# ScalarE in place of VectorE for modulated values and V's weight splits in the first projection

## The chip, the cores and the metric

The kernel runs on one core of one Trainium2 chip. The metric is the device time of one execution in microseconds (us); for a kernel, the median of its runs. The engines are named as in the profile: PE is TensorE (matmuls; PEld are its weight loads), DVE is VectorE, ACT is ScalarE, POOL is GpSimd, and SP issues the DMA transfers.

## The reference

One layer of an encoder, batch 1, 1024 tokens, model width 1024, all in float32. What matters for this change is the beginning:

```python
mod = jnp.dot(jax.nn.silu(c), w_ada[l]) + b_ada[l]
sh_a, sc_a, g_a, sh_m, sc_m, g_m = jnp.split(mod, N_MOD, axis=-1)
h = modulate(rmsnorm(x, g_attn_norm[l]), sh_a, sc_a)
proj = jnp.dot(h, w_in[l])
q_lat, kv_lat, k_rope, ca_qkv = jnp.split(proj, split_pts, axis=-1)
...
x = x + g_a[:, None, :] * mixed
...
x = x + g_m[:, None, :] * jnp.dot(jax.nn.silu(gate) * val, w_down[l])
```

`modulate(h, shift, scale)` is `h * (1 + scale) + shift`. The columns of `w_in` feed two kinds of attention (latent attention, "MLA", and chunked attention over a key band), whose outputs go through one output projection; a gated MLP with a causal convolution follows.

## The kernel before

**Splits.** A float32 product is made on PE as three products of parts. Each operand is split into a rounded part ("hi", type fp32r) and the remainder ("lo", the value minus hi). `gemm3` then issues hi x hi (L154), hi x lo (L155) and lo x hi (L156) into the same PSUM tile. `hi_of(eng, o, i)` makes a rounded part: on ACT as a copy (L77), on POOL, or on DVE as a cast (L81). `lo_of` makes the remainder as a subtraction (L84).

**The opening stage.** The 1024 model dimensions are eight blocks of 128, d = 0 to 7; the 1024 tokens are two halves of 512, h = 0 and 1. The modulation (shift and scale) is not there at the start: its weights `w_ada_a` come in four pairs of blocks, each as four tiles `adaw` of 512 KB (five buffers), and `ada_pair` adds them up on DVE, weighted by silu(c), in eight steps per pair (L271, then L273 seven times) into `adacc`. For each block d, PE sums `adacc` over the partitions with matmuls of one column into `p_ada` (L288), and DVE makes the two columns of `modT` from it (L291 to L293). Two blocks share one pair: blocks 2 and 3 need the second pair, 4 and 5 the third, 6 and 7 the fourth.

For each block and each half, `mod_transpose` has PE transpose four tiles of the normalized x into one PSUM tile `ht_ps` (L228; one buffer for each half, named T and pv). ACT makes the rounded modulated part into `hT[:, 0]` (L231). The full-precision modulated value `hv` is made from the same PSUM tile by the engine that the argument `veng` names: ACT (L234) or DVE (L236). The remainder `hT[:, 1]` is their difference (L237), on DVE or POOL by the argument `leng`. Before the change, half 0 has `hv` on ACT and the remainder on POOL; half 1 has both on DVE. The PSUM buffer of a half is free for the next block when both readings of it are done.

Then PE adds this block's part of the first Q/K projection for all eight token tiles: 24 matmuls with 128x256 outputs into `qk0` (two PSUM tiles, one for each half). When all eight blocks are done, ACT copies `qk0` (L344) and squares it (L346), DVE sums the squares (L349), POOL makes the inverse roots, and DVE multiplies.

**V's weights.** `wv0_load` loads the eight raw chunks of V's weights (`wvr`, 128x256 each) on SP's queue behind the last modulation weight. `wv0_split(k)` makes of chunk k the rounded part, the remainder (POOL), and one column of `ssw0`, the sum of squares over the chunk's columns; before the change the rounded part is a DVE cast (L81) and the sum of squares a DVE multiply-and-reduce (L262). Blocks 4 to 7 split two chunks each. `ssw0` goes into `pow2_scale`, which chooses a power of two for V's float16 form. V's projection on PE (`ipv`) starts directly behind the last matmul of `qk0`, and needs all eight chunks.

**What sets the order.** A scheduler builds one fixed queue for each engine, from priorities and its own estimate of durations. `tc.issue_after(x)` makes it place an instruction behind x; it adds no wait on the chip. `anchor` is a dictionary that remembers the last instruction of a kind for this: `"act"` the last L231, `"lov"` and `"lop"` the last remainder on DVE and on POOL. Since the order follows from estimates, a change in the first stage moves instructions in later stages as well.

**Behind the stage** come the attention parts (to about 630 us), the output projection and normalization, the MLP (from about 716 us) and the down projection.

Of the kernel before, what the change touches and what calls it, by code (L numbers as in the profile page):

```python
# [18 lines left out]
AF = mybir.ActivationFunctionType  # L19
# [3 lines left out]
MUL, ADD, SUB, MIN, MAX = ALU.mult, ALU.add, ALU.subtract, ALU.min, ALU.max  # L23
# [41 lines left out]
def layer_kernel(ctx, tc, I, out):  # L65
    nc = tc.nc
    pe, act, dve, pool, sp = nc.tensor, nc.scalar, nc.vector, nc.gpsimd, nc.sync
# [7 lines left out]
    def hi_of(eng, o, i):  # L75
        if eng == "a":
            act.activation(o, i, AF.Copy)  # L77
        elif eng == "p":
            pool.tensor_scalar(o, i, 1.0, 0.0, op0=MUL, op1=ADD)
        else:  # L80
            dve.tensor_copy(o, i)  # L81

    def lo_of(eng, o, i, hi):
        (pool if eng == "p" else dve).tensor_tensor(o, i, f32(hi), op=SUB)  # L84
# [30 lines left out]
    anchor = {}  # L115
# [10 lines left out]
    hw = right.__enter__()  # L126
# [9 lines left out]
    st = startp.__enter__()  # L136
# [13 lines left out]
    def gemm3(pt, pairs, start=True, stop=True):  # L150

        n = len(pairs)
        for i, (sh, sl, mh, ml) in enumerate(pairs):
            pe.matmul(pt, sh, mh, start=(start and i == 0), stop=False)  # L154
            pe.matmul(pt, sh, ml, start=False, stop=False)  # L155
            last = pe.matmul(pt, sl, mh, start=False, stop=(stop and i == n - 1))  # L156
        anchor["pe"] = last.ins
# [44 lines left out]
    def load_ada(dd, c):  # L202
        w = st.tile([P, 2, 512], F32, name=f"adaw_{dd}_{c}", tag="wa", bufs=5)
        anchor["ada"] = sp.dma_start(w[:], I["w_ada_a"][dd][:, 2 * c:2 * c + 2]).ins
        wada[dd, c] = w
# [10 lines left out]
    for t in range(NT):  # L216
        xt = xs[t]
        junk = st.tile([P, D], mybir.dt.bfloat16, name=f"xj{t}", tag="hv", bufs=2)
# [5 lines left out]
    def mod_transpose(src, k, h, row, pspool, psum_tag, pb, hpool, tag, tmp, nbuf, veng, leng):  # L224

        pt = pspool.tile([P, 512], F32, name=f"ht_ps{row}_{k}_{h}", tag=psum_tag, bufs=pb)
        for j in range(4):
            pe.transpose(pt[:, j * P:(j + 1) * P], src(j), ident[:])  # L228
        pg = hpool.tile([P, 2, 512], F32R, name=f"hT{row}_{k}_{h}", tag=tag, bufs=nbuf)
        a, b = modT[:, row, k:k + 1], modT[:, row + 1, k:k + 1]  # L230
        anchor["act"] = act.activation(pg[:, 0], pt[:], AF.Identity, scale=a, bias=b).ins  # L231
        v = tmp.tile([P, 512], F32, name=f"hv{row}_{k}_{h}", tag="hv", bufs=2)
        if veng == "a":
            act.activation(v[:], pt[:], AF.Identity, scale=a, bias=b)  # L234
        else:
            dve.tensor_scalar(v[:], pt[:], a, b, op0=MUL, op1=ADD)  # L236
        lo = (dve if leng == "v" else pool).tensor_tensor(pg[:, 1], v[:], f32(pg[:, 0]), op=SUB)  # L237
        anchor["lo" + leng] = lo.ins
        return pg

    hT = {}
# [3 lines left out]
    ssw0 = cst.tile([P, ND], F32, name="ssw0")  # L245

    wv0, wv0r = [], []

    def wv0_load():
        with tc.issue_after(anchor["ada"]):  # L250
            for k in range(ND):
                r = st.tile([P, 256], F32, name=f"wv0_r{k}", tag="wvr", bufs=8)
                anchor["sp"] = sp.dma_start(r[:], I["w_v"][0][:, k, :]).ins
                wv0r.append(r)

    def wv0_split(k):
        w = hw.tile([P, 2, 256], F32R, name=f"wv0_s{k}", tag="ws", bufs=16)
        junk = st.tile([P, 512], F32, name=f"wv0_j{k}", tag="wvj", bufs=1)
        with tc.issue_after(anchor["lov"]), tc.issue_after(anchor["lop"]):
            hi_of("v", w[:, 0], wv0r[k][:])  # L260
            lo_of("p", w[:, 1], wv0r[k][:], w[:, 0])
            dve.tensor_tensor_reduce(junk[:, :256], wv0r[k][:], wv0r[k][:], 1.0, 0.0, MUL, ADD,  # L262
                                     accum_out=ssw0[:, k:k + 1])
        wv0.append((w[:, 0], w[:, 1]))

    def ada_pair(dd):
        acc = rtile(f"adacc_{dd}")
        for k in range(ND):
            w = wada[dd, k // 2][:, k % 2]
            if k == 0:  # L270
                dve.tensor_scalar(acc[:], w, cs[:, 0:1], None, op0=MUL)  # L271
            else:
                dve.scalar_tensor_tensor(acc[:], w, cs[:, k:k + 1], acc[:], op0=MUL, op1=ADD)  # L273
        accs[dd] = acc

    ada_pair(0)
    for d in range(ND):
        dd, half = divmod(d, 2)
        if half == 0 and dd + 1 < ND // 2:
            for c in range(4):  # L280
                load_ada(dd + 1, c)
            if dd + 2 == ND // 2:
                wv0_load()
            ada_pair(dd + 1)
        pt = ps.tile([P, 512], F32, name=f"p_ada{d}", tag="mm", bufs=2)
        for i in range(2):
            c0 = half * 256 + i * P
            pe.matmul(pt[:, i:i + 1], accs[dd][:, c0:c0 + P], ones[:, 0:1], start=True, stop=True)  # L288

        tmp = cst.tile([P, 1], F32, name=f"adat{d}", tag="adat", bufs=2)  # L290
        dve.tensor_scalar(tmp[:], pt[:, 0:1], pk[:, C_B + 8 + d:C_B + 9 + d], 1.0, op0=ADD, op1=ADD)  # L291
        dve.tensor_tensor(modT[:, 0, d:d + 1], tmp[:], pk[:, C_GA + d:C_GA + d + 1], op=MUL)
        dve.tensor_tensor(modT[:, 1, d:d + 1], pt[:, 1:2], pk[:, C_B + d:C_B + d + 1], op=ADD)  # L293
        for h in range(2):
            hT[d, h] = mod_transpose(lambda j: xs[4 * h + j][:, d * P:(d + 1) * P], d, h, 0, ps, ("T", "pv")[h], 1,
                                     hw, "hT", st, 16, "v" if h else "a", "v" if h else "p")
        if d >= ND // 2:
            for k in range(2 * d - ND, 2 * d - ND + 2):
                wv0_split(k)
        for t in range(NT):  # L300
            h, j = divmod(t, 4)
            sl = slice(j * P, (j + 1) * P)
            gemm3(qk0[h][:, j * 256:(j + 1) * 256],
                  [(hT[d, h][:, 0, sl], hT[d, h][:, 1, sl]) + wqk[d]], start=(d == 0 and j % 2 == 0), stop=(d == ND - 1 and j % 2 == 1))
# [1272 lines left out]
def build(arrays):  # L1577
    nc = bacc.Bacc("TRN2", target_bir_lowering=False, num_devices=1, dynamic_dma_scratch_size=1024)
    I = {k: nc.dram_tensor(k, v.shape, mybir.dt.from_np(v.dtype), kind="ExternalInput").ap()
         for k, v in arrays.items()}  # L1580
    out = nc.dram_tensor("out_0_dram", (S, D), F32, kind="ExternalOutput").ap()
    with tile.TileContext(nc, schedule_with_timeline_sim=True) as tc, ExitStack() as ctx:
        layer_kernel(ctx, tc, I, out)
    return nc
# [8 lines left out]
```

## Time and profile before

| | us |
|---|---|
| median of 3 runs | 1341.95 |
| lowest, highest | 1338.59, 1342.17 |
| the profiled execution | 1345.32 |
| its span, first to last instruction | 1343.5 |

| engine | busy us in the span | share |
|---|---|---|
| PE | 1223.3 | 91% |
| PEld | 1002.6 | 75% |
| DVE | 1095.6 | 82% |
| ACT | 621.9 | 46% |
| POOL | 579.7 | 43% |

How to read it. All times are of one profiled execution; its mean granted PE clock is 0.948 of full speed. Matmuls are pipelined and their ends are modelled, so a busy PE may still run at half clock; the column PEclk shows that. A row of the timeline gives the start, the duration, the engine, the line, the operation, what it writes and reads, the shapes, and in brackets how long the engine was idle before it and what ended that. A share of busy time is an average over stages with different limits; what a change in one stage is worth is read from that stage.

### The profile page before, as it was taken

Reading aid. Unit: us, or ns where it says so; the run is one execution under the profiler, and the core shown is the slowest. Engines: PE = TensorE matmul, PEld = TensorE weight load, DVE = VectorE, ACT = ScalarE, POOL = GpSimd, SP = SyncE. Lnnn points to the kernel's source line nnn. Section 1 sums busy time; section 2 is a strip of 40 time slices with the busy share of each in tenths; the row PEclk is TensorE's granted clock in tenths of the full one; section 3 lists DMA queues with packets and bytes.
Section 4 is the critical chain, followed back from the end, with each engine's and each line's share of the span. In section 5 each row is a group of like instructions: output and inputs, shape, how many; then the busy total and the mean of one; then the engine's idle time right before and its main releaser. Section 6 shows DMA issues by size and latency. Waiting matters only on the chain.

```text
span 1343.5 us, 18697 instructions
## 1 busy us (share of the span) xinstructions
PE 1223.3 (91%) x6168; PEld 1002.6 (75%) x6168; DVE 1095.6 (82%) x1928; ACT 621.9 (46%) x1132; POOL 579.7 (43%) x610
## 2 busy tenths in 40 slices
PE   4899798998867798896988999999999999999998
PEld 3888587887655576774867888888888886888886
DVE  6977898864679987894989888899999997687667
ACT  4453555443556544552375444444434444433331
POOL 5474656565646763363725444444435431000000
PEclk9899798999797899997998999999999998999999
DMA  8415677944413486779901333333333326943441
GB/s 321 140 32 120 137 173 181 192 124 113 90 30 80 97 166 153 148 153 270 364 32 63 110 113 131 102 107 113 120 116 117 127 96 232 388 154 118 131 160 62
DMA packets 223689, 190.57 MB, mean 142 GB/s; under 512 B 148708, under 2 KB 166884, under 8 KB 223592
## 3 DMA queue, kind: packets, MB, share of 16 engines
q1 hardware_dynamic: 223592, 189.38, 49.5%
q8 instruction: 48, 0.79, 0.2%
q14 instruction: 49, 0.40, 0.1%
HBM read 117.24 MB, written 37.49 MB: 115 GB/s over the span
## 4 chain that ended last, share of the span: by engine, by line
PE 41%; DVE 10%; issue 3%; ACT 2%; DMA 1%; POOL 1%; SPq 0%; DVEq 0%; ACTq 0%; POOLq 0%
PE p L1075 7%; PE p L1077 7%; PE p L1076 7%; PE dnA_P L1404 2%; PE dnA_P L1406 2%; PE dnA_P L1405 2%; PE dnB_P L1406 1%; PE dnB_P L1405 1%; PE dnB_P L1404 1%; DVE u L1246 1%; DVE u L1247 1%; PE dnA L1404 1%; PE op L154 1%; PE dnA L1406 1%; PE dnA L1405 1%
## 5 line engine op out<-in xcount | busy, mean ns | idle before, releaser
L77 ACT ACTIVATE dnP<-dnr 128x1024 fp32r<-128x1024 f32 x73 | 77.5, 1064 | 117.1 <-PE dnA_P L1406 46.4
L1378 DVE TENSOR_TENSOR dnP<-dnr,dnP 128x1024 fp32r<-128x1024 f32 x72 | 87.9, 1223 | 52.5 <-ACT dnP L77 52.5
L73 POOL TENSOR_SCALAR hlm<-Pm,rim 128x512 f16<-128x512 f32 (+3 forms) x96 | 69.3, 732 | 79.8 <-DVE rim L800 21.8
L84 POOL TENSOR_TENSOR wf<-wu,wf 128x512 fp32r<-128x512 f32 x22 | 39.3, 1789 | 116.3 <-ACT wf L77 106.8
L1246 DVE SCALAR_TENSOR_TENSOR u<-c,cvp,u 128x1023 f32<-128x1023 f32 x44 | 65.0, 1519 | 27.8 <-ACT u L1245 27.8
L73 POOL TENSOR_SCALAR hlc<-Pc,ric 128x640 f16<-128x640 f32 (+2 forms) x64 | 49.7, 780 | 61.1 <-ACT Pc L797 15.4
L819 DVE SCALAR_TENSOR_TENSOR hlm<-Pm,rim,hlm 128x512 f16<-128x512 f32 (+3 forms) x96 | 66.7, 706 | 10.3 <-POOL hlm L73 10.1
L797 ACT ACTIVATE Pc<-sc,mc 128x640 f32<-128x640 f32 (+2 forms) x64 | 42.1, 658 | 53.5 <-DVE mc L786 30.6
L1245 ACT ACTIVATE u<-c,cvp 128x1024 f32<-128x1024 f32 x44 | 52.3, 1237 | 28.7 <-DVE c L1338 19.5
L84 POOL TENSOR_TENSOR wb<-wu,wb 128x512 fp32r<-128x512 f32 x22 | 38.5, 1751 | 61.6 <-ACT wb L77 55.5
L797 ACT ACTIVATE Pm<-sm,mm 128x128 f32<-128x128 f32 (+3 forms) x64 | 47.1, 736 | 38.4 <-DVE mm L790 21.1
L1247 DVE SCALAR_TENSOR_TENSOR u<-c,cvp,u 128x1022 f32<-128x1022 f32 x44 | 64.8, 1510 | 0.0
L859 PE MATMUL pvm<-PTm,vt 128*128 128x256 f16 (+1 forms) x320 | 46.6, 298 | 15.4 <-DMA PTm<-hlm 10.7
L819 DVE SCALAR_TENSOR_TENSOR hlc<-Pc,ric,hlc 128x640 f16<-128x640 f32 (+2 forms) x64 | 50.4, 790 | 8.8 <-POOL hlc L73 8.2
L154 PE MATMUL ipq<-wq_s,hT 128*128 128x256 f32 x192 | 56.1, 295 | 0.0
L155 PE MATMUL ipq<-wq_s,hT 128*128 128x256 f32 x192 | 56.0, 293 | 0.0
L859 PEld LDWEIGHTS <-vt 128*128 128x128 f16 x320 | 32.0, 110 | 31.5 <-DMA PTm<-hlm 15.0
L156 PE MATMUL ipq<-wq_s,hT 128*128 128x256 f32 x192 | 55.4, 289 | 0.0
L77 ACT ACTIVATE wc<-ws 128x512 fp32r<-128x512 f32 x21 | 13.3, 632 | 86.0 <-DVE ws L1094 86.0
L1406 PE MATMUL dnA_P<-dnP 128*128 128x512 f32 x132 | 51.3, 389 | 0.0
L1405 PE MATMUL dnA_P<-dnP 128*128 128x512 f32 x132 | 51.3, 389 | 0.0
L1404 PE MATMUL dnA_P<-dnP 128*128 128x512 f32 x132 | 51.2, 389 | 0.0
(434 smaller groups left out, 4429.6 us busy)
## 6 DMA issues: line engine op xcount, KB each, us to landing
wu<-w_up SPq DMA_DIRECT2D x44, 512.0 KB, 3.5
dnr<-g_d SPq DMA_DIRECT2D x73, 256.0 KB, 2.8
aw<-w_ada SPq DMA_DIRECT2D x48, 256.0 KB, 3.6
g_d<-u SPq DMA_DIRECT2D x22, 512.0 KB, 3.0
dnr<-w_down SPq DMA_DIRECT2D x44, 256.0 KB, 5.4
adaw<-w_ada_a SPq DMA_DIRECT2D x16, 512.0 KB, 6.5
x<-x SPq DMA_DIRECT2D x16, 512.0 KB, 9.0
g_d<-gs SPq DMA_DIRECT2D x22, 256.0 KB, 2.7
```

The lines of the kernel that those rows point to most:

```text
L73: pool.tensor_scalar(o, i, s, 1.0, op0=MUL, op1=MUL)
L77: act.activation(o, i, AF.Copy)
L797: act.activation(pr[:, :n], sv, AF.Exp, bias=m[:], scale=-1.0, accum_out=rsum[:, 0:1])
L819: dve.scalar_tensor_tensor(hl[:, w:2 * w], pp, ri[:], hl[:, :w], op0=MUL, op1=SUB)
L859: last = pe.matmul(dst, u.vst(j), mov, start=(x == 0), stop=(x == len(todo) - 1), skip_group_check=True)
L1075: pe.matmul(pt, sh, pg[:, 0], start=(k == 0 and not add), stop=False, skip_group_check=skip)
L1076: pe.matmul(pt, sh, pg[:, 1], start=False, stop=False, skip_group_check=skip)
L1077: last = pe.matmul(pt, sl, pg[:, 0], start=False, stop=(k == 3), skip_group_check=skip)
L1378: r = f(*a, **k)
L1404: pe.matmul(pt, sh, w[:, 0, 0], start=start, stop=False, skip_group_check=add)
L1405: pe.matmul(pt, sh, w[:, 1, 0], start=False, stop=False, skip_group_check=add)
L1406: pe.matmul(pt, sl, w[:, 0, 0], start=False, stop=stop, skip_group_check=add)
```

## The change

Two calls change engine, and with them an order constraint:

```diff
     def wv0_split(k):
         w = hw.tile([P, 2, 256], F32R, name=f"wv0_s{k}", tag="ws", bufs=16)
         junk = st.tile([P, 512], F32, name=f"wv0_j{k}", tag="wvj", bufs=1)
-        with tc.issue_after(anchor["lov"]), tc.issue_after(anchor["lop"]):
-            hi_of("v", w[:, 0], wv0r[k][:])
+        with tc.issue_after(anchor["act"]), tc.issue_after(anchor["lop"]):
+            hi_of("a", w[:, 0], wv0r[k][:])
             lo_of("p", w[:, 1], wv0r[k][:], w[:, 0])
-            dve.tensor_tensor_reduce(junk[:, :256], wv0r[k][:], wv0r[k][:], 1.0, 0.0, MUL, ADD,
-                                     accum_out=ssw0[:, k:k + 1])
+            act.activation(junk[:, :256], wv0r[k][:], AF.Square, accum_out=ssw0[:, k:k + 1])
         wv0.append((w[:, 0], w[:, 1]))
...
             hT[d, h] = mod_transpose(lambda j: xs[4 * h + j][:, d * P:(d + 1) * P], d, h, 0, ps, ("T", "pv")[h], 1,
-                                     hw, "hT", st, 16, "v" if h else "a", "v" if h else "p")
+                                     hw, "hT", st, 16, "a", "v" if h else "p")
```

`hv` of half 1 is made by ACT (L234) instead of DVE (L236), so ACT reads each `ht_ps` twice in both halves. The rounded parts of V's eight weight chunks become ACT copies, and their sums of squares become ACT squares with an accumulator. The remainders stay where they were: half 1's on DVE, half 0's and V's on POOL. The splits are now placed behind the block's last L231 instead of behind its remainder on DVE.

In the built program DVE has 32 instructions fewer (8 hv, 8 casts, 8 multiply-and-reduce and 8 reads of their accumulator) and ACT the 24 that take their place, besides the accumulator reads. In ACT's queue the order from block 4 on is: hT and hv of both halves, cast, square, cast, hT and hv of block 5's first half, square, and so on; the casts and squares of chunks 6 and 7 stand between block 7's last hv and the copies of `qk0`. In DVE's queue, the columns of `modT` for blocks 2 and 3 stand behind two more steps of the next pair's sum than before, those of blocks 4 and 5 behind two fewer. POOL's and SP's queues change by single places in this stage. The queues are dealt differently through the attention parts, and are the same from the MLP on.

## The prediction

> **What bounds the kernel now.** The edit touches only the opening stage, from the start to the first matmul of V, so I read that stage and then asked what carries its end to the kernel's end. The first view is the busy time in stretches of 4 us (columns: length, busy time and count of PE, PEld, DVE, ACT, POOL, then granted clock, DMA share, GB/s).
> ```profile
> core 0: us, PE busy (x) PEld busy (x) DVE busy (x) ACT busy (x) POOL busy (x), PEclk, DMA share, GB/s
> 36.00:40.00 4.00, 3.95 (x21) 3.71 (x22) 4.00 (x12) 0.21 (x1) 0.00 (x0) 0.66 0.68 209
> 40.00:44.00 4.00, 3.50 (x15) 2.74 (x13) 3.93 (x5) 3.77 (x7) 2.69 (x2) 0.50 1.04 367
> 44.00:48.00 4.00, 4.00 (x23) 4.00 (x22) 4.00 (x5) 1.03 (x2) 2.43 (x3) 0.56 0.83 284
> 48.00:52.00 4.00, 4.00 (x35) 3.92 (x35) 3.96 (x12) 1.03 (x2) 0.00 (x0) 1.00 0.63 191
> 52.00:56.00 4.00, 3.33 (x29) 3.12 (x28) 4.00 (x10) 2.64 (x4) 2.61 (x2) 1.00 0.00 0
> 56.00:60.00 4.00, 4.00 (x37) 4.00 (x36) 4.00 (x11) 0.78 (x1) 2.42 (x3) 1.00 0.00 0
> 60.00:64.00 4.00, 3.96 (x34) 3.75 (x33) 4.00 (x10) 2.82 (x5) 2.85 (x3) 1.00 0.02 4
> 64.00:68.00 4.00, 3.29 (x24) 2.65 (x23) 3.93 (x13) 1.52 (x3) 1.59 (x2) 1.00 0.01 2
> 68.00:72.00 4.00, 2.61 (x21) 2.62 (x22) 3.93 (x9) 1.12 (x3) 2.94 (x4) 1.00 0.01 2
> sum 48.00, PE 41.71 PEld 38.54 DVE 47.44 ACT 18.89 POOL 26.34; mean PE 3.48 PEld 3.21 DVE 3.95 ACT 1.57 POOL 2.19
> ```
> DVE is full: 47.44 us of the 48 from 24 to 72, while ACT works 18.89. That makes DVE look like the bound. But PE is nearly full too, and part of its time is a slow clock (0.50 and 0.56 from 40 to 48). From 40 to 72 PE is idle for only 0.50 + 0.67 + 0.04 + 0.71 + 1.39 = 3.3 us. Who makes it idle, in the same 48 us (total, times, longest):
> ```profile
> ACT hT L231 <- DVE modT L292: 12.5, 3, 6.6
> ...
> POOL wv_s L84 <- DVE wv_s L81: 6.2, 7, 2.3
> ...
> PE qk L156 <- POOL hT L237: 2.5, 3, 1.5
> ```
> ACT waits on DVE 12.5 us for modT, and PE waits on what DVE or POOL deliver late. In order of time the stage has these marks:
> ```profile
> 36.05 0.66 PE L228 MATMUL ht_ps<-ident,x 128*128 128x128 f32 x4 [1.74 <-DVE hv L236]
> 39.55 0.22 DVE L292 TENSOR_TENSOR modT<-adat,pk 128x1 f32<-128x1 f32 x2
> 39.79 0.78 ACT L231 ACTIVATE hT<-ht_ps,modT 128x512 fp32r<-128x512 f32 x1 [6.59 <-DVE modT L292]
> 50.72 0.15 DVE L292 TENSOR_TENSOR modT<-adat,pk 128x1 f32<-128x1 f32 x1
> 59.81 0.14 DVE L292 TENSOR_TENSOR modT<-adat,pk 128x1 f32<-128x1 f32 x1
> 68.07 1.26 POOL L237 TENSOR_TENSOR hT<-hv,hT 128x512 fp32r<-128x512 f32 x1
> 69.39 0.39 PE L156 MATMUL qk<-wq_s,hT 128*128 128x256 f32 x1 [1.50 <-POOL hT L237]
> 70.88 1.09 ACT L344 ACTIVATE raw<-qk 128x512 f32<-128x512 f32 x2 [4.19 <-PE qk L156]
> 71.76 0.28 PE L156 MATMUL qk<-wq_s,hT 128*128 128x256 f32 x1
> ```
> modT for blocks d = 2, 4 and 6 appears at 39.55, 50.72 and 59.81; the last PE wait ends on block 7's remainder from POOL; the stage's last matmul starts at 71.76 and V's first follow at once.
>
> **The change part by part.** The groups of the same 48 us (busy, mean ns; idle before), and one row of the first 180 us for ACT's accumulator read:
> ```profile
> L273 DVE SCALAR_TENSOR_TENSOR adacc<-adaw,cs,adacc 128x512 f32<-128x512 f32 x21 | 19.1, 917 | 0.2
> ...
> L231 ACT ACTIVATE hT<-ht_ps,modT 128x512 fp32r<-128x512 f32 x15 | 11.6, 777 | 24.3 <-DVE modT L292 12.5 <-PE ht_ps L228 10.6 <-DVE hb L333 1.1
> ...
> L236 DVE TENSOR_SCALAR hv<-ht_ps,modT 128x512 f32<-128x512 f32 x8 | 6.3, 793 | 0.0
> L237 DVE TENSOR_TENSOR hT<-hv,hT 128x512 fp32r<-128x512 f32 x8 | 6.3, 787 | 0.1
> L81 DVE CAST wv_s<-wv_r 128x256 fp32r<-128x256 f32 x8 | 5.5, 684 | 0.0
> L234 ACT ACTIVATE hv<-ht_ps,modT 128x512 f32<-128x512 f32 x7 | 5.4, 773 | 0.1
> L262 DVE CUSTOM_DVE_ANT_0 wv_j<-wv_r 128x256 f32<-128x256 f32 x8 | 4.4, 553 | 0.0
> ...
> L77 ACT ACTIVATE wq_s<-wq_r 128x256 fp32r<-128x256 f32 x6 | 2.4, 409 | 0.6 <-DMA wq_r<-w_qk 0.6
> ...
> L262 DVE DVE_READ_ACCUMULATOR2_ANT ssw<- 128x1 f32 x8 | 0.6, 78 | 0.0
> ```
> ```profile
> L219 ACT ACTIVATION_READ_ACCUMULATOR xj<-x 128x1 f32 x8 | 1.5, 188 | 0.0
> ```
> Off DVE go eight hv (6.3 us), eight casts (5.5) and eight sums of squares (4.4 + 0.6): 16.8 us. On ACT come eight hv at 0.773 (6.2), eight casts at 0.409 (3.3), and eight squares. A 128x256 square with an accumulator is not on ACT in this trace. Below it lies a cast of that shape, 0.41; above it that cast plus the accumulator read, 0.41 + 0.19 = 0.60; I take 0.60, since the read is always there (4.8 us). So ACT gains 14.3 us and DVE loses 16.8. No DMA is added; in SP's queue, by the built order, two loads of the modulation weights pass one load of Q/K weights, which block 6 needs.
>
> The casts now stand in ACT's queue ahead of hT and hv of blocks 5 to 7, so a late raw V weight would hold those. The eight loads are issued here, and land in 4.3 us:
> ```profile
> 41.62 5.88 SPq L253 DMA_DIRECT2D wv_r<-w_v  x8
> ```
> ```profile
> wv_r<-w_v SPq DMA_DIRECT2D x8, 128.0 KB, 4.3
> ```
> The first is there at about 46.3, the last at 47.5 + 4.3 = 51.8. ACT comes to the first cast after block 4 (47.7 + 3.1 = 50.8), and to the last ones some 15 us later: this wait costs nothing.
>
> The remark on pricing that the rest does not need: the Trainium skill ("ScalarE: Activation LUTs", Rules for kernel authors) sends simple multiplies and adds to VectorE, up to about 3 times faster per element in bf16, which speaks against this change. Here the same operation on the same PSUM tile takes 793 ns on DVE and 773 on ACT, so the trace does not bear the rule out for this shape; by the rule ACT's 6.2 us would stand against some 2 on DVE.
>
> *Block 2.* Two hv (1.6 us) leave DVE ahead of modT 2, but the built order puts two more weight sums L273 there (0.73 to 0.92 each, 1.5). It stays near 39.5: no gain.
>
> *Block 4.* Ahead of its modT two more hv go (1.6), and two weight sums now stand behind it (1.5). So 50.72 becomes about 47.6.
>
> *PE.* Its work from 40 on is the same matmuls. Where DVE was late it waited 3.3 us; where ACT, with new work, is late it will wait instead. ACT's load per block is 2 x 0.777 + 2 x 0.773 = 3.1 us, and between blocks 4 and 7 two casts and two squares, 2.0: 5.1 against PE's 36 matmuls at 4.00/37 us, 3.9. So ACT becomes the slower of the two for three blocks. From 47.7 it needs 3 x 5.1 + 3.1 = 18.4, to 66.1. Its last value but one (hT 7, second half) is there at 65.3; PE then has two matmuls and two groups of ten, 22 x 0.12 us (the spacing at 1.00 clock, 4.00/37 to 0.12) = 2.6, which gives 67.9 or, with the remainder's L237 at 0.787, 68.1. PE alone cannot do it before 71.8 - 3.3 = 68.5. The later one counts: 68.5, a gain of 3.3 us; no PE gap is left to win more at this clock.
>
> *Behind the blocks.* The casts and squares of the last two weight chunks stand on ACT ahead of the copies of qk0 (L344): 2 x 0.41 + 2 x 0.60 = 2.0 after 66.1. The copies start at about 68.2 rather than 70.88, 2.7 earlier. They feed the Q/K normalization, for which PE has V's first product as cover (48 matmuls, 48 x 0.12 = 5.8 us); without it the loss is 3.3 - 2.7 = 0.6. POOL's eight wv remainders need the casts earlier than now: 6.2 us of its waits on DVE go, but none of them reached PE.
>
> *Sum:* -3.3 at the stage's end, of which 2.7 to 3.3 pass on; I take -3.0. From 72 to 140 PE is busy for 64.71 of 68 us at full clock, so an earlier start there is an earlier end:
> ```profile
> 72.00:140.00 68.00, 64.71 (x487) 58.46 (x485) 52.51 (x166) 30.36 (x69) 36.42 (x44) 1.00 0.37 87
> ```
> The profiled execution took 1345.32 us (span 1343.5), so it would take 1342.3. It lies 3.4 above the median of the runs, 1341.95; with the same step off, that gives 1339.0. About 0.3%, 4.0 us, is what a measurement of this kernel can tell from no change, so the forecast is a gain that is just under it.
>
> **The rivals.**
>
> *ACT only takes DVE's place.* If modT 4 does not come earlier, because the weight sums run long when POOL works (917 ns in the mean), ACT starts block 4 at 50.97 as now: 50.97 + 18.4 = 69.4, less 0.8, plus 2.6 gives 71.2, and the late copies of qk0 eat the rest. The time stays: 1342. For it: ACT's 5.1 us per block. Against it: DVE is rid of 16.8 us.
>
> *A stall in attention that was not there (slower).* The build orders instructions by its own estimate of times, and in the changed order DVE, ACT, POOL and PE are re-dealt all through attention; from the MLP on nothing moves. In the order of PE single instructions move by up to 216 places. What one bad order costs can be read where it happens now:
> ```profile
> 204.99 0.58 PE L154 MATMUL ipv<-wv_s,hT 128*128 128x256 f32 x1 [5.02 <-DVE hlc L819]
> ```
> ```profile
> 200.00:210.00 10.00, 4.76 (x17) 3.81 (x17) 7.20 (x21) 7.10 (x23) 7.46 (x9) 0.73 0.70 127
> 210.00:220.00 10.00, 10.00 (x63) 8.40 (x63) 9.76 (x22) 5.24 (x14) 7.27 (x8) 0.76 0.91 239
> 220.00:230.00 10.00, 10.00 (x74) 8.60 (x73) 7.84 (x31) 5.53 (x14) 6.85 (x11) 1.00 0.77 172
> ```
> PE waits 5.02 us for DVE's hlc, and then the clock is down: 17 + 63 = 80 matmuls took 20 us, and at the rate of the next 10 us (74) they take 10.8. So the stall costs 9.2. It decides from one more such stall on: 1341.95 - 3.0 + 9.2 = 1348.2. For it: DVE's order is re-dealt in just that stage. Against it: the same dealing can also remove the stall that is there.
>
> *More than the forecast.* The clock of 40 to 48 is granted at about half after the PE wait that ends at 36.05 (1.74 us, on hv, which ACT now makes). There 15 + 23 matmuls took 8 us, 0.5 of it idle; at 37 in 4 us they take 4.1, so 3.4 more are to be had, 1341.95 - 3.0 - 3.4 = 1335.6. Against it: modT 2 stays at 39.5, and PE, done sooner with blocks 0 and 1, then waits for it. The Trainium skill ("TensorE: Matmul & The Clock Gate", Part 1) has the half clock come after an idle window of some 3.4 us; here the clock fell behind a gap of 1.74 us, so the gap need not be that long, and by either a shorter gap is no sure cure.
>
> **How the numbers follow.** Forecast 0.36 (1336.5 to 1341), half of it beyond 4.0 us; ACT in DVE's place 0.13; the stall 0.33; more than the forecast 0.18. Faster by over 0.3%: 0.18 + 0.18 = 0.36. Within: 0.18 + 0.13 = 0.31. Slower: 0.33. The range takes in the slow clock's end with some luck in the dealing (1331) and the stall (1348.2, up to 1350); the likeliest case alone is 1336.5 to 1341.
>
> **What would show it.** Right: the last qk matmul at 68 to 69; modT of block 4 near 47.5 and of block 2 still near 39.5; ACT busy for some 14 us more from 24 to 72 and DVE for some 17 less; PE's last waits there on ACT's hT. The square with its read at 0.4 to 0.6. Wrong: the last qk matmul at 71 or later (ACT as bound), full clock from 40 to 48 (more), or a stage that ends 3 us earlier while the span does not, with new PE waits on DVE or ACT between 140 and 630 (the stall).

## The result, and the profile after

| kernel | runs | median us | lowest, highest us |
|---|---|---|---|
| before | 8 | 1342.99 | 1338.59, 1347.01 |
| after | 8 | 1355.62 | 1348.08, 1358.63 |

After to before is 1.0079, with a 95% interval of 1.0060 to 1.0098. The change makes the kernel slower by 0.8%, some 10.6 us (0.0079 x 1343; the ratio and its interval are not those of the two medians, which lie 12.6 us apart), where the prediction had it 3 us faster. The profiled execution of after is its fastest run, 1348.08 us (span 1346.3); a second one, of the same kernel in the experiments (called "the changed kernel, again"), took 1356.00 (span 1354.2) and lies nearer to the median. Both are read below. The changed kernel's text is one line shorter: what stands behind L263 in the kernel before has a number that is one less (L292 is L291, L344 is L343).

**The edited stage is faster.** The busy time of after in stretches of 4 us from 24 to 72 (columns as in the prediction: length, busy time and count of PE, PEld, DVE, ACT, POOL, granted clock, DMA share, GB/s):
```profile
...
36.00:40.00 4.00, 2.73 (x24) 2.53 (x23) 3.96 (x12) 0.41 (x1) 0.00 (x0) 1.00 0.73 246
40.00:44.00 4.00, 3.40 (x17) 2.96 (x18) 3.90 (x6) 4.00 (x8) 2.00 (x2) 0.73 0.96 329
44.00:48.00 4.00, 4.00 (x19) 4.00 (x20) 4.00 (x9) 1.14 (x4) 3.41 (x3) 0.50 0.81 279
48.00:52.00 4.00, 4.00 (x34) 4.00 (x32) 3.89 (x6) 2.28 (x4) 1.29 (x1) 0.91 0.56 172
...
64.00:68.00 4.00, 4.00 (x34) 3.89 (x34) 1.16 (x2) 3.97 (x12) 2.92 (x3) 1.00 0.01 2
68.00:72.00 4.00, 4.00 (x36) 4.00 (x35) 2.43 (x4) 3.75 (x8) 2.29 (x3) 1.00 0.00 0
sum 48.00, PE 44.51 PEld 42.87 DVE 37.58 ACT 32.62 POOL 28.00; mean PE 3.71 PEld 3.57 DVE 3.13 ACT 2.72 POOL 2.33
```
The sums are to be set beside those of before, PE 41.71, DVE 47.44, ACT 18.89: DVE is no longer full, ACT does 13.7 us more, and PE, which was idle 3.3 us between 40 and 72, is idle there for 0.6, all of it before 44. The half clock has not gone; it comes later, behind a PE gap that now ends at 40.42. Read in windows of 1 us, half speed is granted from 41.9 to 48.7, where it was 37.3 to 47.5 before. Its length is not what moves the end of the stage: in two of the experiments below, the stage of before had it for 6.8 us only (38.5 to 45.3) and ended at 72.0, and the changed stage had it for 10.2 us (38.0 to 48.2) and ended at 67.8. The marks of the stage in the timeline of after (start, duration, engine, line, what; in brackets the idle time before and its end):
```profile
39.34 0.22 DVE L291 TENSOR_TENSOR modT<-adat,pk 128x1 f32<-128x1 f32 x2
40.42 0.39 PE L154 MATMUL qk<-wq_s,hT 128*128 128x256 f32 x1 [1.68 <-ACT hT L231]
46.75 0.75 DVE L291 TENSOR_TENSOR modT<-adat,pk 128x1 f32<-128x1 f32 x2
51.72 0.78 ACT L231 ACTIVATE hT<-ht_ps,modT 128x512 fp32r<-128x512 f32 x1 [1.72 <-PE ht_ps L228]
67.15 1.06 ACT L343 ACTIVATE raw<-qk 128x512 f32<-128x512 f32 x2
67.74 0.28 PE L156 MATMUL qk<-wq_s,hT 128*128 128x256 f32 x1
```
The last `qk` matmul starts at 67.74 instead of 71.76, 4.0 us earlier, and the copies of `qk0` at 67.15 instead of 70.88. Nearly all of that is gained from block 4 on: the 97th of the 192 `qk` matmuls, with which block 4 begins, starts at 52.72, where it was 52.83. The groups of after from 24 to 72 that answer to those of before (busy, mean ns; idle before):
```profile
L237 DVE TENSOR_TENSOR hT<-hv,hT 128x512 fp32r<-128x512 f32 x8 | 7.7, 958 | 7.3 <-ACT hv L234 7.3
...
L234 ACT ACTIVATE hv<-ht_ps,modT 128x512 f32<-128x512 f32 x15 | 11.7, 779 | 0.2 <-DVE hT L237 0.2
L262 ACT ACTIVATE wv_j<-wv_r 128x256 f32<-128x256 f32 x8 | 3.4, 424 | 0.0
L77 ACT ACTIVATE wv_s<-wv_r 128x256 fp32r<-128x256 f32 x8 | 3.1, 425 | 0.0
...
L262 ACT ACTIVATION_READ_ACCUMULATOR wv_j<-wv_r 128x1 f32 x8 | 1.6, 206 | 0.0
```
`hv` takes ACT 779 ns, the cast 425, the square 424 and its read 206.

**The time is lost later.** The start of the last or first matmul of a stage, each from the first and last starts of the tile's matmuls in that profile:

| mark, us | before | after | the changed kernel, again |
|---|---|---|---|
| last `qk` (opening stage ends) | 71.8 | 67.7 | 68.2 |
| last `ipq` (Q/K projection ends) | 283.0 | 279.5 | 280.5 |
| last `mp` (latent projections end) | 349.5 | 349.4 | 348.1 |
| last `ku` (latent keys and values are up) | 465.1 | 466.2 | 465.4 |
| first `op` (output projection starts) | 627.0 | 631.8 | 633.7 |
| last `op` | 673.9 | 679.4 | 686.7 |
| span | 1343.5 | 1346.3 | 1354.2 |

Up to 280 us the gain is there as forecast. From 280 to 465 all of it is lost in both profiles, between the last `ku` and the first `op` (latent attention, with the matmuls `oc` of the output projection's chunked part between) the changed kernel loses another 3.7 to 6.4 us, and in the second profile 6.1 more inside the output projection. Four profiles in the experiments below share the changed operations and before's order up to `op`, and they show how far a single execution can be read: from the last `ipq` to the last `ku` they take 179.5 to 183.8 us (182.1 before, 186.7 and 184.9 here), from there to the first `op` 160.5 to 162.2 (161.9 before). So only the second loss is well clear of what differs by chance. No line of these stages is touched by the diff. What PE waits for there differs. The waits of PE from 460 to 640 (total us, times, longest), before,
```profile
PE pvm L859 <- DMA PTm<-hlm: 8.3, 7, 3.4
PE sm L771 <- ACT Pm L797: 5.8, 8, 1.7
PE pvm L859 <- DVE om L869: 4.4, 2, 2.8
PE op L154 <- ACT oh L77: 2.4, 1, 2.4
PE mk_ps L697 <- DVE mq_0l L706: 2.0, 1, 2.0
...
PE oc L154 <- ACT ch L77: 0.2, 1, 0.2
```
and in the changed kernel, again:
```profile
PE pvm L858 <- DMA PTm<-hlm: 11.6, 9, 4.1
PE sm L770 <- ACT Pm L796: 8.0, 9, 2.1
PE pvm L858 <- DVE om L868: 5.8, 2, 4.0
PE oc L154 <- ACT ch L77: 2.9, 1, 2.9
PE pvm L858 <- DVE hlm L818: 2.2, 1, 2.2
PE mq_ps L696 <- DVE mk L709: 1.1, 1, 1.1
...
```
The three largest waits are there again, longer; some others have grown (`oc` on `ch` from 0.2 to 2.9 us) and some are gone (`mk_ps` on `mq_0l`). PE stands more often at a transposed probability (`PTm`, by DMA), an exponential (`Pm`, ACT) or a rounded operand (`ch`, ACT) that is not there yet. In the output projection of that second profile one wait makes most of the difference:
```profile
662.47 0.80 PE L156 MATMUL op<-wo,ol 128*128 128x512 f32 x1 [5.37 <-POOL ol L84]
```
The remainder `ol` of a token tile is made by POOL only at 660.41, behind a normalization and remainders of the MLP's weights in its queue. The same kernel's first profile has 1.0 us of such waits.

The one large stall that the prediction had quoted (5.02 us at 204.99) has at the same time become shorter, as this row of after shows:
```profile
198.99 0.58 PE L154 MATMUL ipv<-wv_s,hT 128*128 128x256 f32 x1 [2.71 <-ACT wv_s L77]
```
But PE's waits from 180 to 240 are not fewer in all: 5.8 us after, 5.2 before.

### The profile page after: what moved, and what is told of

Same layout as the page of the kernel before. It is cut to its first block, busy times and chain, and to the rows that moved or that the text cites. A ratio compares the mean times of both kernels' runs of the same rounds, so it can differ in the third digit from the quotient of the medians.

```text
span 1346.3 us, 18685 instructions
## 1 busy us (share of the span) xinstructions
PE 1221.5 (91%) x6168; PEld 1003.0 (75%) x6168; DVE 1087.1 (81%) x1896; ACT 634.6 (47%) x1164; POOL 579.0 (43%) x610
## 5 line engine op out<-in xcount | busy, mean ns | idle before, releaser
L1245 DVE SCALAR_TENSOR_TENSOR u<-c,cvp,u 128x1023 f32<-128x1023 f32 x44 | 61.1, 1429 | 27.5 <-ACT u L1244 26.2
L84 POOL TENSOR_TENSOR wb<-wu,wb 128x512 fp32r<-128x512 f32 x22 | 43.7, 1987 | 70.5 <-ACT wb L77 55.9
L858 PEld LDWEIGHTS <-vt 128*128 128x128 f16 x320 | 31.6, 107 | 38.5 <-issue 18.4
```

Source lines behind the costliest of these rows:

```text
L858: last = pe.matmul(dst, u.vst(j), mov, start=(x == 0), stop=(x == len(todo) - 1), skip_group_check=True)
L1245: dve.scalar_tensor_tensor(u[:, 1:], c[:, :S - 1], cvp[:, cv + 1:cv + 2], u[:, 1:], op0=MUL, op1=ADD)
```

## The experiments

**The theory and its rivals.** Theory 1: the loss comes from the order of the queues behind the stage, which the scheduler deals differently since its estimates of the first stage have changed; the new operations themselves are a gain. Rival: the new operations do harm that shows only later (PE reaches the same work earlier, and so collides with other transfers or meets a colder clock). To part them, operations and order were exchanged. Both kernels trace the same instructions with the same numbers behind the last `qk` matmul, so the order of one can be forced on the other: for each engine a list of instruction numbers is stored, and each instruction is made to be placed behind the one ahead of it in the list, with an edge that orders the queue and puts no wait on the chip:

```diff
+def pin_order(nc, tc):
...
+    traced = {i.name: i for i in nc.cur_bb.bb.instructions}
+    info = mybir.DependencyInfo(mybir.DependencyClass.NoSync, mybir.DependencyReason.DATA)
+    for text in ORDER.values():
+        seq = np.cumsum(np.frombuffer(zlib.decompress(base64.b85decode(text)), "<i2").astype(int))
+        seq = [f"I-{k}" for k in seq if f"I-{k}" in traced]
+        for a, b in zip(seq, seq[1:]):
+            if traced[a].engine == traced[b].engine:
+                tc.add_manual_dep(traced[b], a, info, reason="pin_order")
...
         layer_kernel(ctx, tc, I, out)
+        pin_order(nc, tc)
     return nc
```

### Operations and order exchanged

The changed kernel with the order of before behind the opening stage (`ORDER`, not printed here, holds before's lists):

> The changed kernel, with every instruction traced behind the last qk0 matmul put, on each engine, in the order that the kernel before has; the opening stage is the changed one. Theory 1 (the re-dealt order of attention costs the time; the opening stage gains 4 us, its last qk matmul at 67.7 instead of 71.8): about 1343 - 4 = 1339, between 1337 and 1341. Theory 2 (the new opening stage itself harms what follows, by starting transfers and waits at other times): it stays near the changed kernel, 1352 to 1358. Theory 3 (the gain of the stage is lost at the first later wait, and the rest is order): 1342 to 1344.

The kernel before with the changed kernel's order behind the opening stage:

> The kernel before, with every instruction traced behind the last qk0 matmul in the order that the changed kernel has; the opening stage is that of before. Theory 1: the whole loss and none of the gain, 1355.6 + 4 = about 1360, between 1355 and 1363. Theory 2: as before, 1341 to 1345. Theory 3: as the changed kernel, 1354 to 1357.

The changed kernel as it is, beside them on the same chip:

> The changed kernel once more, beside the two others on the same chip, for a second profile: its runs so far lie between 1348 and 1359 and the profiled one was the fastest. All theories: 1350 to 1359; where the profile is of a run near 1356 it shows where the 7 us more than in the first profile go: theory 1 expects them in the attention parts, behind 280 us, and none before 72 us.

| operations | order behind the stage | ratio to before | 95% interval | last `qk` | ku to op |
|---|---|---|---|---|---|
| changed | before's | 0.9984 | 0.9966 to 1.0002 | 67.7 | 160.5 |
| before's | changed | 1.0108 | 1.0078 to 1.0139 | 72.0 | 168.6 |
| changed | changed | 1.0068 | 1.0044 to 1.0091 | 68.2 | 168.3 |

"ku to op" is the time in us from the start of the last `ku` matmul to that of the first `op` matmul; before itself has 161.9. The order alone, without one changed operation, costs 1.08%, 14.5 us of 1343.3. With the order held, the changed operations do not cost anything. So the rival falls. Two things stay open here. The median of the first exchange, 1341.7, lies between the ranges of theory 1 (to 1341) and theory 3 (from 1342), so that run does not say whether the stage's gain reaches the end. And no run forces a kernel's own order on it, so what the forcing itself costs was not measured; before's operations in the changed order come out 0.40% above the changed kernel as it is, and the 4.0 us of the stage are 0.30%, which leaves little room for it. The ends of the stretch, as the tile rows of three profiles give them (times min/median/max ns, first and last start us), before,
```profile
L156 PE MATMUL ku<-wk,latT x16: 391/397/628, 372.5 to 465.1; 128*128 128x512 f32 x16
...
L154 PE MATMUL op<-wo,oh x64: 387/389/797, 627.0 to 673.4; 128*128 128x512 f32 x64
```
changed operations in before's order,
```profile
L156 PE MATMUL ku<-wk,latT x16: 391/397/628, 367.4 to 461.3; 128*128 128x512 f32 x16
...
L154 PE MATMUL op<-wo,oh x64: 387/389/794, 621.8 to 670.3; 128*128 128x512 f32 x64
```
and before's operations in the changed order:
```profile
L156 PE MATMUL ku<-wk,latT x16: 391/397/629, 369.1 to 467.3; 128*128 128x512 f32 x16
...
L154 PE MATMUL op<-wo,oh x64: 388/389/796, 635.9 to 686.0; 128*128 128x512 f32 x64
```
The last pair shows the loss by itself: with the opening stage of before, `ku` ends 2.2 us later than before, and `op` starts 8.9 us later. The matmuls themselves are no slower (the medians are 397 and 389 ns in all three).

### Where in the order

The lists were then joined: one kernel's order up to a mark, the other's behind it, always on the changed operations. In outline, for one direction:

```diff
-ORDER = lists(before)
+ORDER = lists(before[:cut] + [i for i in changed if i not in before[:cut]])
```

Cut behind the last `ku` matmul, in both directions, and at the first `op` matmul:

> The changed kernel, with each engine's instructions behind the first projection held in the order of the kernel before up to the last ku matmul (about 460 us), and in the changed kernel's own order from there on. Theory A (what costs is the order of the latent attention and output projection, 465 to 690 us; the order ahead of it costs only the 3 us of the mp stage): the ratio to before is 1.003 to 1.007, nearly that of the changed kernel (1.0068), last ku matmul near 461, first op matmul 628 to 634, and PE's waits for PTm from the DMA and for Pm from ACT in 460 to 700 are together 18 us or more (14.9 with the old order throughout, 19.6 to 20.9 with the new one). Rival B (the early part of the new order leaves the later stages with less work to fill gaps with, so the order up to ku decides): the ratio is 0.997 to 1.001, first op matmul 621 to 624.

> The complement: the changed kernel's own order up to its last ku matmul, the order of the kernel before from there on. Theory A: the ratio is 0.998 to 1.002, first op matmul 622 to 628. Rival B: 1.004 to 1.007, first op matmul 630 to 635. If the loss is shared, both hybrids stand between, near 1.002 to 1.004.

> As the first, but the order of the kernel before lasts to its first op matmul (about 622 us), and only what stands behind it is in the new order. Theory A with the loss in the attention: the ratio is 0.997 to 1.000, first op matmul near 622, c_g end near 703. Rival C (the order of the output projection and what follows costs by itself, as its length of 49 to 53 us against 47 in the profiles may say): the ratio is 1.002 to 1.005, and first to last op matmul takes 50 us or more.

Cut inside latent attention, behind the last score matmul of head 3's first token half, in both directions:

> The changed kernel with the order of the kernel before up to the last score matmul of the fourth head's first token half (sm of head 3, about 515 us), and its own new order behind it. If the loss sits in the first half of the latent attention (where the new order spends the oc matmuls early and then waits 1.6 to 2.9 us for their operand from ACT), the ratio is 0.997 to 1.001 and the first op matmul comes 621 to 625. If it sits in the second half or is spread over both, 1.002 to 1.006 and 627 or later.

> The complement: the new order up to the last score matmul of head 3's first token half, the order of the kernel before behind it. First half guilty: ratio 1.004 to 1.008, first op matmul 628 or later. Second half guilty: 0.999 to 1.003 (the new order up to ku by itself cost 1.0031), first op matmul 622 to 627. Spread: between the two.

| order up to the cut, then | cut | ratio | 95% interval | ku to op | PE's waits in it |
|---|---|---|---|---|---|
| before's, changed | last `ku` | 1.0069 | 1.0046 to 1.0092 | 172.6 | 36.2 |
| before's, changed | head 3 | 1.0024 | 1.0003 to 1.0046 | 170.3 | 30.0 |
| before's, changed | first `op` | 0.9974 | 0.9951 to 0.9996 | 162.0 | 24.0 |
| changed, before's | last `ku` | 1.0031 | 1.0013 to 1.0048 | 163.4 | 25.8 |
| changed, before's | head 3 | 1.0066 | 1.0040 to 1.0093 | 170.0 | 32.9 |

The last column is the sum over all rows of PE's waits between those two matmuls; before has 25.6, the first exchange (changed operations, before's order) 21.3, the second (before's operations, changed order) 31.7, and the changed kernel, again, 31.1.

What follows. The order behind the first `op` is not at fault: with only that in the changed order nothing is lost, and the output projection took 46.9 us from first to last start, as before. The rival of an output projection that costs by itself falls; its 53.0 us in the second profile of the changed kernel is mostly the single wait of 5.37 us shown above. The latent attention between `ku` and `op` is where most of the loss shows: with before's order there the stretch takes 160.5 to 163.4 us in each profile, with any other 165.6 to 172.6. It is not the only place: with the changed order up to `ku` alone the stretch takes 163.4 us, but the last `ku` comes at 469.5 instead of 465.1. Which part of the order costs has no single answer. Replacing before's order from the end, the part behind head 3 costs 0.50% (0.9974 to 1.0024), the part between `ku` and head 3 another 0.45% (to 1.0069), and the part up to `ku` nothing more (1.0068). Replacing it from the front, all up to `ku` costs 0.47% (0.9984 to 1.0031), the part between `ku` and head 3 a further 0.35% (to 1.0066), and the part behind it nothing more (1.0068). Each of these steps is uncertain by some 0.3%. So the expectations came true in one direction and not in the other: before's order up to `ku` did as theory A has it, its complement lies between theory A and rival B, and the first half of the attention is guilty alone only when the order is replaced from the front. That would fit a price that depends on what the queues hold when a piece of order begins; no run shows this by itself.

The longest of these stretches, before's order to `ku` and the changed one behind, shows what the price is made of (its profile is of that kernel's fastest run, 1347.16 us, where the median is 1354.04). Its waits of PE from 460 to 640:
```profile
PE sm L770 <- ACT Pm L796: 10.4, 9, 3.3
PE pvm L858 <- DMA PTm<-hlm: 10.1, 7, 3.1
PE pvm L858 <- DVE om L868: 6.2, 2, 4.1
PE pvm L858 <- DVE qn L467: 5.5, 1, 5.5
PE oc L154 <- ACT ch L77: 1.6, 1, 1.6
...
```
and those of changed operations in before's order throughout:
```profile
PE pvm L858 <- DMA PTm<-hlm: 8.0, 7, 3.3
PE sm L770 <- ACT Pm L796: 6.9, 8, 1.7
PE op L154 <- ACT oh L77: 3.6, 2, 2.7
PE mk_ps L696 <- DVE mq_0l L705: 2.0, 1, 2.0
PE ku L154 <- ACT uqr L631: 2.0, 1, 2.0
PE pvm L858 <- DVE om L868: 1.6, 1, 1.6
...
```
The stretch is 172.6 - 160.5 = 12.1 us longer, and PE's waits in it are 36.2 - 21.3 = 14.9 longer. No single wait carries that: it is 3.5 here on ACT's exponentials, 4.6 there on DVE's `om`, 5.5 on what the profile names as a normalization on DVE (`qn`).

The expectation that the waits for `PTm` and `Pm` alone would tell the orders apart did not hold: together they are 14.9 us with before's order and 20.5 in this hybrid, but 22.3 in the kernel with the changed order up to `ku` and before's behind it, whose stretch took 163.4. The sum of all waits between the last `ku` and the first `op` does tell them apart: 21.3 to 26.7 us in each profile with before's order there, 29.0 to 36.2 with any other.

### One half of the change at a time

Only the modulated values on ACT:

```diff
-                                     hw, "hT", st, 16, "v" if h else "a", "v" if h else "p")
+                                     hw, "hT", st, 16, "a", "v" if h else "p")
```

> Only the modulated values of the second token half go to ACT; V's casts and squares stay on DVE; the order behind is what the planner makes of it. Opening stage: it takes 6.3 of the 16.8 us off DVE, so the last qk matmul comes 1.2 to 3 us before the 71.8 of before, at 69 to 70.6. Whole: if any re-dealt order is worse than the one before, 1.002 to 1.010; if only the particular order of the changed kernel is (its oc matmuls spent early, its mk late), this one, whose first-half sequence of sm, pvm and oc stands nearer to before's, gives 0.996 to 1.001.

Only V's casts and sums of squares on ACT:

```diff
-        with tc.issue_after(anchor["lov"]), tc.issue_after(anchor["lop"]):
-            hi_of("v", w[:, 0], wv0r[k][:])
+        with tc.issue_after(anchor["act"]), tc.issue_after(anchor["lop"]):
+            hi_of("a", w[:, 0], wv0r[k][:])
...
-            dve.tensor_tensor_reduce(junk[:, :256], wv0r[k][:], wv0r[k][:], 1.0, 0.0, MUL, ADD,
-                                     accum_out=ssw0[:, k:k + 1])
+            act.activation(junk[:, :256], wv0r[k][:], AF.Square, accum_out=ssw0[:, k:k + 1])
```

> Only V's casts and sums of squares go to ACT; the modulated values stay on DVE. Opening stage: 10.5 of 16.8 us off DVE, last qk matmul 68.5 to 70. Whole: its planned order spends the oc matmuls of the first half even earlier than the changed kernel's (48 of them before the first three score tiles of head 3 are through), so the order's price should come back: 1.004 to 1.010 if that is the cause; 0.996 to 1.001 if the price is that of the changed kernel's order alone and not of early oc.

| on ACT | ratio | 95% interval | last `qk` | ku to op |
|---|---|---|---|---|
| modulated values | 1.0065 | 1.0039 to 1.0090 | 68.9 | 166.6 |
| V's casts and squares | 1.0035 | 1.0016 to 1.0054 | 68.4 | 170.1 |
| both (the changed kernel, again) | 1.0068 | 1.0044 to 1.0091 | 68.2 | 168.3 |

The halves shorten the stage by 2.9 and 3.4 us, at the upper end of what was expected of each and nearly what both do together, although PE is still idle there: 2.2 and 1.0 us from 40 to the stage's end, against 3.3 before and 0.6 with both. And each half, with the order that the scheduler deals for it, is slower as a whole. The profile of V's half is of its fastest run, 1343.36 us, where the median is 1351.17; even there the stretch from `ku` to `op` is 8.2 us longer than before. The idea that it is the early use of the `oc` matmuls that costs finds no support: by 500 us, 70 of the 192 have started with V's half, 60 in the changed kernel, 48 before and 33 with the modulated values, and both the earliest and the latest lose. V's half, at 1.0035, lies between its two expected ranges. With modulated values only, a good part of the loss lies at another place, as these rows of its profile show:
```profile
L156 PE MATMUL ipq<-wq_s,hT x192: 278/283/682, 99.9 to 277.0; 128*128 128x256 f32 x192
...
L156 PE MATMUL mp<-wm_h,hT x64: 345/353/548, 277.5 to 355.2; 128*128 128x416 f32 x64
```
Its Q/K projection ends at 277.0, 6 us earlier than before's 283.0, and its latent projections at 355.2, 5.7 later than before's 349.5: with that order PE takes 78 us from the one to the other instead of 66.5. Part of that is other work that now stands there: 338 matmuls start between the two marks instead of 304, 32 of the 34 more belonging to the chunked attention (`pvc`, `sc`). Three orders were dealt anew, the changed kernel's and these two, and all three kernels are slower, with the loss at different places.

### The changed operations in the good order, once more

> The changed operations with the order of the kernel before throughout, once more, since 0.9984 [0.9966, 1.0002] left open whether the opening stage's gain reaches the end. If the 4.1 us that the last qk matmul gains is carried as forecast (3 us): ratio 0.996 to 0.999. If it is lost on the way: 0.999 to 1.002.

> The order of the kernel before up to the first op matmul, the changed kernel's own order behind it, once more, after 0.9974 [0.9951, 0.9996]. If the order behind 622 us is indifferent: the same ratio as the run beside it within 0.2%. If the new order is better there: 0.996 to 0.998 with the run beside it at 0.998 or above.

Before's order throughout gave 0.9973 (0.9956 to 0.9990), before's order up to the first `op` 0.9993 (0.9978 to 1.0008). The two differ by 0.20%, just what was allowed, and by 0.10% the other way in the first pair, so the order behind 622 us is indifferent as far as these runs can tell. The mean of the four runs with the changed operations and before's order up to `op` (0.9984, 0.9974, 0.9973, 0.9993) is 0.9981, a gain of 2.6 us of 1344; from the four intervals, taken as independent, 1.3 to 3.8 us. That is the version that beats both kernels, by less than 0.3%.

## Why the prediction was wrong

**Right, by its steps.** *Off DVE and on ACT:* ACT gained 13.7 us from 24 to 72, where 14.3 was worked out. The square with its read costs 424 + 206 = 630 ns, just above the bound of 0.60. DVE lost 9.9 us in that window instead of 17. DVE's next work (three sums of squares of `qk0`, 2.0 us, and others) came into the window because the stage ended earlier, L237 took 1.4 us more, and the sum of durations had been too large from the start: an instruction's record overlaps the next one's (after the change one of 0.21 us starts at 38.30 and the next at 38.42), so busy time falls by less than the durations that leave. *The V weights' loads:* no wait on them came up. *Block 2* stayed, 39.34 for its `modT`. *Block 4:* `modT` starts at 46.75 and is there at 47.5; 47.6 was worked out. *The half clock* stayed too, and that its length can change by 3.4 us without moving the end of the stage, as shown above, speaks against the price of "more than the forecast", which took all of that time for a gain. *Behind the blocks:* the copies of `qk0` came at 67.15, a little earlier than 68.2.

**A term slightly off.** *PE and ACT:* ACT was not late. It is busy from 52 to 68 almost without a gap, but what it waited for at 51.72 was PE's transposes, 1.72 us, and PE itself has no idle time from 44 on. So the last `qk` matmul came at 67.74, where 68.5 was worked out, and "PE's last waits there on ACT's hT" did not show. "PE alone cannot do it before 68.5" was off by 0.8. The sum took away all of PE's idle time from 40 on, 3.3 us. Of that, 0.5 lies ahead of block 4, where 0.6 is still idle after the change; behind it were 2.8, and PE gained 3.9 there. What the other 1.1 us are was not followed up.

*The remark on pricing* sets a figure that it gives for bf16 against float32 tiles, so 793 and 773 ns neither confirm nor refute it. Nothing in the sum rests on it.

**The step that failed.** "From 72 to 140 PE is busy for 64.71 of 68 us at full clock, so an earlier start there is an earlier end." Up to 280 us this held: the last `ipq` came 3.5 us earlier. It did not hold for the rest, because the sum carried the gain through stages whose order the same text says is dealt anew, at a price of nothing. What the runs showed in its place is that the new order has a price of its own. With the order held, the sum is about right: 2.6 us measured against 3.0, though 4.0 us were gained at the stage's end and not 3.3. With the order as built, 14.5 us come on top (the order alone, on before's operations), together 11.9 slower; the measured 10.6, with an interval of 8.1 to 13.2, agrees.

**The rival that came true** was the stall in attention, and with it the sign that the prediction named for it: a stage that ends 3 us earlier while the span does not, with new waits behind 140 us. The cause it names, the order dealt anew, was right, and its size and form were not. It was priced as one stall like the one at 204.99, 9.2 us, from the slow clock behind it. What came is many waits of up to 5.5 us, most of the added ones between the last `ku` and the first `op` (31.1 us in all in the second profile of the changed kernel, 25.6 before), and the stall that served as the price became shorter in the changed order. It had 0.33, with the argument against it that a new dealing can as well remove a stall. It did shorten that one; but of three orders dealt anew, three were slower as a whole, by 0.35 to 0.79%. The waits of before would have told more than its longest stall: between the last `ku` and the first `op` PE waits 25.6 us of 161.9, in many pieces, so a sixth of that stretch hangs on what other engines deliver in time, and that is what another order can make worse. The prediction looked at 72 to 140, where PE is full, and at one stall, and at nothing behind 230.

## What to carry to other kernels

Where a scheduler deals the queues from its estimates, an edit has two prices: what it does at its place, and what the new order costs everywhere behind it. They can be measured apart by holding the order of one kernel on the operations of the other, and a gain of 0.2% can vanish in a dealing that is worth 1%. Before such an edit is judged, the built orders should be compared over the whole kernel, and the stages in which PE waits often for other engines, not those in which it is full, show where a new order can cost.

## What the runs showed of the hardware that was not expected

DVE's remainders L237, with the same operands and shape, took 787 ns in the mean before and 958 after, though their medians hardly differ (678 and 692). Two of the eight took 1.76 and 1.77 us after, and one 1.59 before. Each of these three started while POOL was already working on a remainder of the other half:
```profile
43.82 1.32 POOL L237 TENSOR_TENSOR hT<-hv,hT 128x512 fp32r<-128x512 f32 x1 [0.89 <-ACT hv L234]
...
43.91 1.77 DVE L237 TENSOR_TENSOR hT<-hv,hT 128x512 fp32r<-128x512 f32 x1
```
The other thirteen took 0.62 to 0.69 us. POOL was idle when each of them began, or started its own subtraction only 0.34 us later or more. So of these sixteen, those that find POOL already at such work are the long ones. That the one causes the other is not shown; no run was made to test it.

The sum of squares on ACT costs half as much again for reading the accumulator, 206 ns behind 424. And a higher mean granted clock was no sign of a faster kernel: it was 0.953 in both profiles of the changed kernel and 0.948 in that of before. The time was lost in PE's gaps: of the span, PE was not busy for 120.2 us before and for 124.8 and 132.5 in the two profiles of the changed kernel.
